# Gated MLP in three parts: the second product's accumulation gets a priority, and the third part rotates six tiles of stored weight combinations in place of four

## The chip, the cores and the metric

The kernel runs on one core of one Trainium2 chip. The metric is the device time of one execution in microseconds (us); the time before is the median of three runs.

## The reference, cut to what matters

The layer mixes 2064 rows (16 meta tokens and 2048 inputs) with RWKV-7 heads and attention heads, adds the result to the stream, and applies a gated MLP with a causal convolution of width three. The change touches the MLP alone:

```
def conv_ffn(u, w_up, conv_w, conv_b, w_down):
    hid = u @ w_up                                   # (rows, 1024) @ (1024, 5632)
    hid = (hid * conv_w[0] + shift_right(hid, 1) * conv_w[1]
           + shift_right(hid, 2) * conv_w[2] + conv_b)
    gate, val = jnp.split(hid, 2, axis=-1)           # 2816 each
    return (jax.nn.silu(gate) * val) @ w_down        # (rows, 2816) @ (2816, 1024)

h = h + conv_ffn(rms_norm(h, norm2_w[layer]), w_up[layer], ...)
return h[:, N_META:]
```

## The kernel before

Phase one (mixers and output projection) fills about half of the time and is not touched. Phase two, the MLP, works through the 2048 rows in three **parts** (`PARTS = [384, 384, 256]`); a part is two halves of that many rows, so the third part has 512 rows. All products are in float32 split into a high and a low tile, so that one product is three matmuls per 128 of its inner dimension (`mm3`).

Within a part, a loop runs over 22 column tiles **f** of the hidden layer, gate and value together. For each f the first product (`up_products`) is computed as seven products of half size, on combinations of the four quarters of the weights and of the input (Strassen's scheme in Winograd's form). The program calls them 0 to 6 by operand; on TensorE they stand in the order 0, 1, 4, 3, 5, 6, 2 and are written P0, P1, P4, P3, P5, P6, P2 here. One product is 12 matmuls into one PSUM bank (tag `up`, 4 banks). Its weights lie in a tile `o` of 128 x 1024 float32 (high and low half, 512 KB), and all `o` tiles share a rotation of `OPB` = 4 buffers:

- P0, P1 and P6 use quarters of the raw weights: `wraw` is loaded (512 KB for the first tile, 256 KB for the second, lines 1048 and 1050), ScalarE rounds it to the high half (line 1068) and GpSimd subtracts to get the low half (line 1069).
- P4, P3, P5 and P2 use combinations. The first part computes them and stores the finished `o` tiles in DRAM (`kept`); the second and third part only load them (line 1066).

VectorE and ScalarE combine the seven results, apply the convolution and the gate, and write `gh` and `gl`. The weights of the second product come as `wraw` too (line 152), and ScalarE and GpSimd split them into `dh` and `dl` (lines 155, 156), one buffer for each of two tags' halves.

The second product (`down`) takes two f at a time: after the up products of f = 2, 4, 6 and so on, TensorE runs the 48 matmuls `dn` of the two f before, six for each bank of 128 x 512, and VectorE adds each bank to the running sum `acc` (line 1031).

Operand tiles of the inputs (`ah`, `al`, seven each, `PARTS[i] + 2` columns wide) sit in a pool of their own that is closed and opened again when the part's size changes, so that in the third part they take 57,792 bytes of a partition where they took 86,464 before. Between the parts (here called the **transition**) the last `down` of a part is computed beside the loading, transposing and combining of the next part's input; its sums go out (line 1033) and the next part's `acc` tiles come in (line 983).

All DMAs are issued by SyncE (SP) in one order. The order of every engine is set by a scheduler that builds a timeline ahead of the run and takes, among what is ready, the instruction of the lowest priority number; matmuls of the products are pinned to the order in which they are written. A rotation of n buffers means that an `o` tile's load, or its rounding on ScalarE, waits until TensorE has finished the product that stands n places before it.

Of the kernel before, what the change touches and what calls it, by code (L numbers as in the profile page):

```python
# [9 lines left out]
F32R = mybir.dt.float32r  # L10
I32 = mybir.dt.int32
AF = mybir.ActivationFunctionType
ALU = mybir.AluOpType
# [23 lines left out]
PARTS = [384, 384, 256]  # L37
HMAX = max(PARTS)

UB, TWB, RAWB, OPB, GHB, TB, CB, DB = 2, 5, 3, 4, 3, 2, 1, 2  # L40
WBUF, QKB = 5, 2
GN = 256


# [47 lines left out]
class K:  # L92
# [222 lines left out]
    def begin(self, g):  # L315
# [3 lines left out]

        xh = sp.tile([128, 8, GN], F32R, tag="xh", name="xh")  # L320
        xl = sp.tile([128, 8, GN], F32R, tag="xl", name="xl")
        if n < GN:
            nc.gpsimd.memset(xh[:, :, n:].bitcast(F32), 0.0)
# [12 lines left out]
    def outputs(self, tag, bufs):  # L336

        return [self.sp.tile([128, 4, GN], F32R, tag=tag + p, name=tag + p, bufs=bufs) for p in "hl"]

# [45 lines left out]
    def duo(self, d):  # L385

        sp, nch = self.sp, self.nch
        return dict(
            gt=sp.tile([128, 2, GN], F32, tag=f"gt{d}", name="gt"),
            gb=sp.tile([128, 2, GN], F32, tag=f"gb{d}", name="gb"),  # L390
            wc=sp.tile([128, 2, 4], F32, tag=f"wc{d}", name="wc"),
# [550 lines left out]
    def phase2(self):  # L942


        tc, nc, a = self.tc, self.nc, self.a
        V, A, P = nc.vector, nc.scalar, nc.gpsimd
        cols = self.cols
        self.qa, self.qf = Queue(tc), Queue(tc)
        with ExitStack() as es:
            pool = lambda name, bufs=1, **kw: es.enter_context(tc.tile_pool(name=name, bufs=bufs, reuse_waits="tile", **kw))  # L950
            up = pool("u2")
            self.psum = Pools(pool("dn2", 4, space=PSUM), up=(pool("up2", 4, space=PSUM), "up"))
            nw = up.tile([128, D], F32, name="nw")
            nc.sync.dma_start(nw, a["n2"].unsqueeze(0).to_broadcast([128, D]))

            self.halo = up.tile([128, 2, 2, 4, 2], F32, name="halo")

            self.tail = up.tile([128, NFT, 2, 2], F32, name="tail")

            self.kp, self.kept = es.enter_context(tc.tile_pool(name="kp2", bufs=1, space=DRAM)), {}  # L960
            wp, sp = pool("w2"), pool("s2")
            lp, ac = pool("l2", side="right"), pool("a2", side="right")
            oes = es.enter_context(ExitStack())

            def operands(i):

                if i and PARTS[i] == PARTS[i - 1]:
                    return ops
                oes.close()
                op = oes.enter_context(tc.tile_pool(name="o2", bufs=1, reuse_waits="tile"))  # L970
                return [[op.tile([128, 4, PARTS[i] + 2], F32R, name=f"a{p}{o}") for p in "hl"] for o in range(7)]

            ops = operands(0)
            dpool = Pools(lp, up=(wp, "wraw"))
            r0 = 0
            self.begin2(0, 0, up, nw, ops)
            for i, half in enumerate(PARTS):
                N = half if i else half + 2
                nb = half // 64
                acc = []  # L980
                for b in range(nb):
                    acc.append(ac.tile([128, D], F32, tag=f"acc{b}", name=f"acc{b}"))
                    nc.sync.dma_start(acc[b], self.h2[r0 + 2 + b * 128:r0 + 130 + b * 128])
                grp = []
                for f in range(NFT):
                    gh = lp.tile([128, 2 * HMAX], F32R, tag="gh", name="gh", bufs=GHB)
                    gl = lp.tile([128, 2 * HMAX], F32R, tag="gl", name="gl", bufs=GHB)
                    cs = self.up_products(f, N, up, wp, sp, ops)
                    for t in range(2):
                        ts = []  # L990
                        for z in range(2):
                            c = cs[2 * t + z]
                            o = sp.tile([128, HMAX], F32, tag=f"t{z}", name=f"t{z}", bufs=TB)[:, 0:half]
                            j = 2 * f + z
                            A.activation(o, c[:, 2:half + 2], AF.Identity, bias=cols[:, C_CB + j:C_CB + j + 1],  # L995
                                         scale=cols[:, C_CW0 + j:C_CW0 + j + 1])
                            V.scalar_tensor_tensor(o, c[:, 1:half + 1], cols[:, C_CW1 + j:C_CW1 + j + 1], o,  # L997
                                                   op0=ALU.mult, op1=ALU.add)
                            V.scalar_tensor_tensor(o, c[:, 0:half], cols[:, C_CW2 + j:C_CW2 + j + 1], o,  # L999
                                                   op0=ALU.mult, op1=ALU.add)  # L1000
                            ts.append(o)
                        A.activation(ts[0], ts[0], AF.Silu)
                        V.tensor_tensor(ts[0], ts[0], ts[1], op=ALU.mult)
                        hs = slice(t * half, t * half + half)
                        A.activation(gh[:, hs], ts[0], AF.Copy)  # L1005
                        P.tensor_tensor(gl[:, hs], ts[0], gh[:, hs].bitcast(F32), op=ALU.subtract)  # L1006
                    grp.append((gh, gl, self.wsplit(dpool, a["wdn"][f], [128, 1024], "d", RAWB, DB)))
                    if f == NFT - 1:
                        if i == len(PARTS) - 1:
                            self.down(grp[:-1], acc, r0, False)  # L1010
                            grp = grp[-1:]
                        if i < len(PARTS) - 1:
                            ops = operands(i + 1)
                            self.begin2(i + 1, r0 + 2 * half, up, nw, ops)
                        self.down(grp, acc, r0, True)
                    elif len(grp) == 3:
                        self.down(grp[:2], acc, r0, False)
                        grp = grp[2:]
                r0 += 2 * half

    def down(self, grp, acc, r0, last):

        nc = self.nc
        for b, t in enumerate(acc):
            bs = slice(b * 128, b * 128 + 128)
            for h in range(2):
                hs = slice(h * 512, h * 512 + 512)
                ps = self.psum.tile([128, 512], F32, tag="dn", name="dn")
                for e, (gh, gl, (wh, wl)) in enumerate(grp):
                    self.mm3(ps, gh[:, bs], gl[:, bs], wh[:, hs], wl[:, hs], e == 0, e == len(grp) - 1)  # L1030
                nc.vector.tensor_tensor(t[:, hs], t[:, hs], ps, op=ALU.add)  # L1031
            if last:
                nc.sync.dma_start(self.out[r0 + b * 128:r0 + b * 128 + 128], t)

    def up_products(self, f, N, up, wp, sp, ops):


        nc = self.nc
# [21 lines left out]

        def product(o, w):

            t = wp.tile([128, 2, 4, 128], F32R, tag="o", name="o", bufs=OPB)
            hi, lo = t[:, 0], t[:, 1]
            if w is None:
                nc.sync.dma_start(t.bitcast(F32), self.kept[o, f])
            else:
                A.activation(hi, w, AF.Copy)  # L1068
                P.tensor_tensor(lo, w, hi.bitcast(F32), op=ALU.subtract)  # L1069
                if o in (2, 3, 4, 5):  # L1070
                    d = self.kept[o, f] = self.kp.tile([128, 2, 4, 128], F32, tag=f"k{o}_{f}", name="kept2")
                    nc.sync.dma_start(d, t.bitcast(F32))
            ps = self.psum.tile([128, 512], F32, tag="up", name="up")[:, 0:N]
            xh, xl = ops[o]
            for k in range(4):
                self.mm3(ps, hi[:, k, :], lo[:, k, :], xh[:, k, 0:N], xl[:, k, 0:N], k == 0, k == 3)
            return ps
# [13 lines left out]
        t1 = comb(b12, b11)  # L1091
        t2 = comb(b22, t1)
        p1 = product(0, b11)
        tu, u = tile_("cu")
        A.activation(u, p1, AF.Copy)
        p2 = product(1, b21)
        t11, c11 = tile_("c11")
        before(t11, tail[:, 0])
        tt(c11, p2, u, op=add)
        p6 = product(4, t2)  # L1100
        tt(u, p6, u, op=add)
        p5 = product(3, t1)
# [125 lines left out]
```

## Time and profile before

| | |
|---|---|
| median of 3 runs | 3096.91 us (3095.21 to 3106.47) |
| the profiled execution | 3101.82 us, span 3100.0 us |
| granted TensorE clock over the span | 0.953 of full speed |
| TensorE, VectorE, ScalarE, GpSimd busy | 91%, 68%, 38%, 36% |
| HBM traffic | 484 MB read, 99 MB written |

The span begins with the first instruction and ends with the last; times of rows count from its start. A busy share is a mean over stages that are limited by different things, so that the rows below are taken from the stretch that the change touches.

### The profile page before, as it was taken

The page shows a single profiled execution, that of the slowest core. Times are in us where ns is not written, and L with a number is a line of the kernel's source. Part 1 is how long each engine was busy: PE and PEld are TensorE (multiplying, and loading weights), DVE is VectorE, ACT ScalarE, POOL GpSimd, SP SyncE. Part 2 cuts the span into 40 slices and gives each one's busy share as a digit, 9 for nine tenths or more (in the row PEclk, how much of TensorE's full clock was granted, in tenths as well). Part 3 has the DMA queues.
Part 4 walks back from the last instruction along what each step waited for, and adds up shares of the span by engine and source line. Part 5 has one row for each costly group of instructions (what it writes and reads, how often), then busy time and mean ns, then how long its engine had stood idle before and what let it go on. Part 6 is the DMA issues. An engine that isn't in the chain of part 4 may idle for free.

```text
span 3100.0 us, 55199 instructions
## 1 busy us (share of the span) xinstructions
PE 2834.1 (91%) x19749; PEld 2396.3 (77%) x19749; DVE 2105.8 (68%) x6008; ACT 1188.0 (38%) x2758; POOL 1107.3 (36%) x1246
## 2 busy tenths in 40 slices
PE   6789898989999999999859999999899999989998
PEld 5567586777777776777548898888899999888887
DVE  5576766667666766666758878787655655766666
ACT  3344433334343433333234443434433333433343
POOL 3322311111111111111146665656444444554554
PEclk8799999989999999999969999999999999999999
DMA  6676677557676767776754343434644444565564
GB/s 216 211 213 187 208 233 233 179 166 231 183 242 183 242 186 226 194 228 192 246 209 156 146 153 133 156 129 162 232 149 139 155 156 140 189 215 177 201 212 159
DMA packets 302198, 586.43 MB, mean 189 GB/s; under 512 B 150570, under 2 KB 154266, under 8 KB 301924
## 3 DMA queue, kind: packets, MB, share of 16 engines
q1 hardware_dynamic: 301924, 582.90, 58.0%
q8 instruction: 157, 2.57, 0.3%
q14 instruction: 117, 0.96, 0.1%
HBM read 483.98 MB, written 98.79 MB: 188 GB/s over the span
## 4 chain that ended last, share of the span: by engine, by line
PE 61%; DVE 15%; DMA 13%; issue 3%; ACT 3%; SPq 3%; POOL 1%; DVEq 0%; ACTq 0%; POOLq 0%
PE up L86 17%; PE dn L86 13%; PE g L86 12%; PE o L86 5%; DMA o<-kept 4%; PE po L86 3%; SPq L587 2%; DMA wraw<-in_wup 2%; PE ma L86 2%; DVE t L997 2%; PE ps L86 2%; DVE tw L1058 2%; DMA w<-kept 2%; DVE t L999 1%; DMA nt<-nd 1%
## 5 line engine op out<-in xcount | busy, mean ns | idle before, releaser
L86 PE MATMUL up<-ah,o 128*128 128x386 f32 (+2 forms) x3696 | 882.7, 324 | 49.9 <-DMA o<-kept 29.0
L86 PEld LDWEIGHTS up<-ah,o 128*128 128x128 f32 x3696 | 652.4, 192 | 61.6 <-issue 11.6
L86 PE MATMUL up<-al,o 128*128 128x386 f32 (+2 forms) x1848 | 596.9, 323 | 6.9 <-DVE al L913 6.9
L86 PE MATMUL g<-xh,w 128*128 128x256 f32 x2016 | 425.8, 301 | 18.7 <-ACT w L170 7.3
L86 PEld LDWEIGHTS g<-xh,w 128*128 128x128 f32 x2016 | 334.7, 198 | 51.6 <-issue 19.8
L86 PEld LDWEIGHTS up<-al,o 128*128 128x128 f32 x1848 | 354.8, 192 | 8.8 <-DVE al L913 7.7
L1031 DVE TENSOR_TENSOR acc<-acc,dn 128x512 f32<-128x512 f32 x360 | 242.4, 684 | 114.9 <-PE dn L86 113.9
L86 PE MATMUL dn<-dh,gh 128*128 128x512 f32 x704 | 279.7, 397 | 29.0 <-DVE acc L1031 26.4
L1069 POOL TENSOR_TENSOR o<-wraw,o 128x512 fp32r<-128x512 f32 x198 | 269.5, 1361 | 99.0 <-ACT o L1068 72.2
L86 PE MATMUL g<-xl,w 128*128 128x256 f32 x1008 | 300.2, 298 | 3.1 <-DVE xl L145 3.1
L86 PE MATMUL dn<-dh,gl 128*128 128x512 f32 x704 | 276.6, 393 | 0.7 <-POOL gl L1006 0.7
L86 PE MATMUL dn<-dl,gh 128*128 128x512 f32 x704 | 276.3, 393 | 0.0
L156 POOL TENSOR_TENSOR dl<-wraw,dh 128x1024 fp32r<-128x1024 f32 x66 | 158.7, 2424 | 203.3 <-ACT dh L155 203.3
L997 DVE SCALAR_TENSOR_TENSOR t<-c,cols,t 128x384 f32<-128x384 f32 (+1 forms) x198 | 169.7, 858 | 79.5 <-ACT t L995 77.4
L86 PEld LDWEIGHTS g<-xl,w 128*128 128x128 f32 x1008 | 199.7, 198 | 14.6 <-issue 6.6
L1006 POOL TENSOR_TENSOR gl<-t,gh 128x384 fp32r<-128x384 f32 (+1 forms) x132 | 134.8, 1021 | 145.4 <-ACT gh L1005 145.4
L592 DVE TENSOR_TENSOR tm<-nt,tt 128x60 f32<-128x60 f32 (+36 forms) x558 | 128.9, 231 | 83.2 <-DMA w<-kept 28.3
L86 PEld LDWEIGHTS dn<-dh,gh 128*128 128x128 f32 x704 | 133.1, 189 | 65.4 <-DVE acc L1031 36.0
L676 POOL TENSOR_TENSOR sw<-S,wc 128x128 f32<-128x128 f32 x66 | 28.5, 432 | 421.1 <-DVE S L677 314.8
L1068 ACT ACTIVATE o<-wraw 128x512 fp32r<-128x512 f32 x198 | 121.8, 625 | 132.4 <-PE up L86 117.5
L995 ACT ACTIVATE t<-c,cols 128x384 f32<-128x384 f32 (+1 forms) x198 | 125.9, 667 | 106.9 <-DVE c L1112 102.1
L86 PE MATMUL g<-w,xh 128*128 128x256 f32 (+3 forms) x544 | 151.7, 362 | 13.9 <-ACT w L170 8.3
(283 smaller groups left out, 5672.3 us busy)
## 6 DMA issues: line engine op xcount, KB each, us to landing
w<-kept SPq DMA_DIRECT2D x448, 512.0 KB
o<-kept SPq DMA_DIRECT2D x176, 512.0 KB
wraw<-in_wup SPq DMA_DIRECT2D x88, 512.0 KB
kept<-o SPq DMA_DIRECT2D x88, 512.0 KB
wraw<-in_wdn SPq DMA_DIRECT2D x66, 512.0 KB
kept<-w SPq DMA_DIRECT2D x56, 512.0 KB
wraw<-in_wup SPq DMA_DIRECT2D x44, 256.0 KB
xt<-in_x SPq DMA_DIRECT2D x16, 512.0 KB
```

The costliest lines, as they stand in the source:

```text
L86: self._pin(self.nc.tensor.matmul(*args, **kw))
L156: nc.gpsimd.tensor_tensor(lo, raw, hi.bitcast(F32), op=ALU.subtract)
L587: nc.sync.dma_start(nt[p0:p0 + H], ndv[:, b * 32:b * 32 + 32, b * 32:b * 32 + 32])
L592: V.tensor_tensor(t, bc(nt[0:np_, s, s + 1:32], j, 1), tt[0:np_, 0:j, s:s + 1].to_broadcast([np_, j, m]), op=ALU.mult)
L995: A.activation(o, c[:, 2:half + 2], AF.Identity, bias=cols[:, C_CB + j:C_CB + j + 1], scale=cols[:, C_CW0 + j:C_CW0 + j + 1])
L997: V.scalar_tensor_tensor(o, c[:, 1:half + 1], cols[:, C_CW1 + j:C_CW1 + j + 1], o, op0=ALU.mult, op1=ALU.add)
L999: V.scalar_tensor_tensor(o, c[:, 0:half], cols[:, C_CW2 + j:C_CW2 + j + 1], o, op0=ALU.mult, op1=ALU.add)
L1006: P.tensor_tensor(gl[:, hs], ts[0], gh[:, hs].bitcast(F32), op=ALU.subtract)
L1031: nc.vector.tensor_tensor(t[:, hs], t[:, hs], ps, op=ALU.add)
L1058: V.tensor_tensor(t, x, y, op=ALU.subtract)
L1068: A.activation(hi, w, AF.Copy)
L1069: P.tensor_tensor(lo, w, hi.bitcast(F32), op=ALU.subtract)
```

## The change

Two edits. The VectorE add of a `down` bank into `acc` is issued under a priority raised by 400. And the tiles `o` of the third part, the only one that is smaller than `HMAX`, are taken from the pool of the operand tiles, in a rotation of six; the four buffers of the first two parts stay where they are and idle in the third.

```
+DOWN = 400
...
                 op = oes.enter_context(tc.tile_pool(name="o2", bufs=1, reuse_waits="tile"))
+
+                self.oplace = (op, OPB + 2) if PARTS[i] < HMAX else (wp, OPB)
                 return [[op.tile([128, 4, PARTS[i] + 2], F32R, name=f"a{p}{o}") for p in "hl"] for o in range(7)]
...
-                nc.vector.tensor_tensor(t[:, hs], t[:, hs], ps, op=ALU.add)
+                with self.tc.high_priority(DOWN):
+                    nc.vector.tensor_tensor(t[:, hs], t[:, hs], ps, op=ALU.add)
...
-            t = wp.tile([128, 2, 4, 128], F32R, tag="o", name="o", bufs=OPB)
+            pool, bufs = self.oplace
+            t = pool.tile([128, 2, 4, 128], F32R, tag="o", name="o", bufs=bufs)
```

What this does to the order of instructions: nothing moves on any engine before the transition from the second to the third part. There, VectorE's adds change places with neighbours by a few rows; in the rounds after it VectorE's order is the same as before but for a few rows of the first two f. TensorE's matmuls differ only in where 8 of the 32 transposes of the transition stand. The rest moves on ScalarE, GpSimd and SP in the third part. Line numbers of the changed kernel are one to five higher.

SP at the transition: `o_29835`, `o_29851`, `o_29869` and `o_29904` are the loads for P4, P3, P5 and P2 of the third part's first f, `wraw_29956` and `wraw_29958` the raw weights of its second f, `out` the sums that leave and `acc` those that come in. Before:

```order
L1066 DMA o_29835<-kept2_19919 128x1024
L1048 DMA wraw_29956<-in_wup 128x1024
L1066 DMA o_29851<-kept2_19938 128x1024
L891 DMA u_29632<-h2_60 128x1024
L891 DMA u_29645<-h2_60 128x1024
L1033 DMA out_0<-acc0_25013 128x1024
...
L1033 DMA out_0<-acc5_25023 128x1024
L1066 DMA o_29869<-kept2_19960 128x1024
L1050 DMA wraw_29958<-in_wup 128x512
L1066 DMA o_29904<-kept2_20000 128x1024
```

Now:

```order
L1071 DMA o_29835<-kept2_19919 128x1024
L1071 DMA o_29851<-kept2_19938 128x1024
L892 DMA u_29632<-h2_60 128x1024
L1071 DMA o_29869<-kept2_19960 128x1024
L892 DMA u_29645<-h2_60 128x1024
L1052 DMA wraw_29956<-in_wup 128x1024
L1054 DMA wraw_29958<-in_wup 128x512
L1037 DMA out_0<-acc0_25013 128x1024
...
L1037 DMA out_0<-acc5_25023 128x1024
L1071 DMA o_29904<-kept2_20000 128x1024
```

The load for P5 and the second half of the raw weights moved from behind the six outgoing sums to ahead of them.

GpSimd at the transition: `o_29798`, `o_29816` and `o_29887` are the low halves for P0, P1 and P6 of the third part's first f; `gl_29388` is one of the low halves that the last `down` of the second part needs. Before:

```order
L1069 TENSOR_TENSOR o_29798<-wraw_29794,o_29798 128x512
L1119 COPY tail_19620<-c22_29479 128x2
L1069 TENSOR_TENSOR o_29816<-wraw_29794,o_29816 128x512
L1085 COPY c22_29479<-c12_29461 128x2
L1118 COPY tail_19620<-cu_29409 128x2
L1085 COPY c12_29866<-tail_19620 128x2
L1006 TENSOR_TENSOR gl_29388<-t0_29519,gh_29387 128x384
```

Now:

```order
L1124 COPY tail_19620<-c22_29479 128x2
L1090 COPY c22_29479<-c12_29461 128x2
L1123 COPY tail_19620<-cu_29409 128x2
L1074 TENSOR_TENSOR o_29798<-wraw_29794,o_29798 128x512
L1074 TENSOR_TENSOR o_29816<-wraw_29794,o_29816 128x512
L1090 COPY c12_29866<-tail_19620 128x2
L1074 TENSOR_TENSOR o_29887<-wraw_29796,o_29887 128x512
L1009 TENSOR_TENSOR gl_29388<-t0_29519,gh_29387 128x384
```

Two conversions moved behind the copies, a third one came in, and all three now stand right ahead of `gl`.

GpSimd in a round of the third part, from the end of a `down` on: `o_30437` is for P6 of the f that now begins (A), `o_30510`, `o_30528` and `o_30599` are for P0, P1 and P6 of the next (B). Before:

```order
L156 TENSOR_TENSOR dl_30275<-wraw_30272,dh_30274 128x1024
L156 TENSOR_TENSOR dl_30501<-wraw_30498,dh_30500 128x1024
L1085 COPY cu_30364<-c11_30382 128x2
L1069 TENSOR_TENSOR o_30437<-wraw_30346,o_30437 128x512
L1085 COPY c11_30544<-tail_19620 128x2
L1069 TENSOR_TENSOR o_30510<-wraw_30506,o_30510 128x512
L1119 COPY tail_19620<-c22_30434 128x2
L1069 TENSOR_TENSOR o_30528<-wraw_30506,o_30528 128x512
```

Now:

```order
L157 TENSOR_TENSOR dl_30275<-wraw_30272,dh_30274 128x1024
L157 TENSOR_TENSOR dl_30501<-wraw_30498,dh_30500 128x1024
L1090 COPY cu_30364<-c11_30382 128x2
L1074 TENSOR_TENSOR o_30510<-wraw_30506,o_30510 128x512
L1074 TENSOR_TENSOR o_30528<-wraw_30506,o_30528 128x512
L1090 COPY c11_30544<-tail_19620 128x2
L1124 COPY tail_19620<-c22_30434 128x2
```

The conversion for A's P6 left this place (it is done before the `down` now), and those for B's P0 and P1 follow directly on the two `dl`.

## Rows read from the trace of the kernel before

**Rows 1.** The page's head and its busy times by engine.

```profile
span 3100.0 us, 55199 instructions
...
PE 2834.1 (91%) x19749; PEld 2396.3 (77%) x19749; DVE 2105.8 (68%) x6008; ACT 1188.0 (38%) x2758; POOL 1107.3 (36%) x1246
```

**Rows 2.** Chain that ended last, third part: start, length, what, how many.

```profile
2706.22 2.68 PE up L86 x23
2708.90 6.39 DMA o<-kept
2715.43 6.92 PE up L86 x36
...
2748.14 10.90 PE dn L86 x48
...
3023.96 4.53 PE up L86 x36
...
3062.42 10.93 PE dn L86 x48
3073.34 8.60 PE up L86 x72
```

**Rows 3.** Groups of instructions, 2740 to 3080 us: busy, mean; idle before, its releasers.

```profile
L86 PE MATMUL up<-ah,o 128*128 128x256 f32 x1079 | 205.9, 288 | 28.3 <-DMA o<-kept 24.2 <-DVE cu L1101 1.9 <-DVE t L1003 1.0
```

**Rows 4.** TensorE in order of time: start, length; in brackets idle before, releaser.

```profile
2688.32 0.51 PE L86 MATMUL dn<-dh,gl 128*128 128x512 f32 x1 [0.35 <-POOL gl L1006]
...
3004.90 0.28 PE L86 MATMUL up<-ah,o 128*128 128x256 f32 x1
...
3014.40 0.36 PE L86 MATMUL up<-ah,o 128*128 128x256 f32 x1 [0.75 <-DMA o<-kept]
...
3021.38 0.36 PE L86 MATMUL up<-ah,o 128*128 128x256 f32 x1 [1.03 <-DVE t L1003]
...
3023.96 0.36 PE L86 MATMUL up<-ah,o 128*128 128x256 f32 x1 [0.92 <-DMA o<-kept]
```

**Rows 5.** SP's DMA issues in one round, in order of time.

```profile
2994.19 12.65 SPq L1066 DMA_DIRECT2D o<-kept  x2
...
3009.41 0.32 SPq L1066 DMA_DIRECT2D o<-kept  x1
...
3013.67 2.75 SPq L1066 DMA_DIRECT2D o<-kept  x2
...
3017.52 3.18 SPq L1066 DMA_DIRECT2D o<-kept  x2
```

**Rows 6.** Stretches: busy PE, PEld, DVE, ACT, POOL; granted clock, DMA share, GB/s.

```profile
2683.00:2707.00 24.00, 22.20 (x115) 17.93 (x114) 23.63 (x37) 12.47 (x22) 14.58 (x13) 1.00 0.68 250
2706.22:2748.14 41.92, 34.88 (x253) 34.16 (x253) 23.77 (x45) 17.07 (x34) 22.90 (x32) 0.88 0.71 246
3006.00:3007.00 1.00, 1.00 (x11) 1.00 (x10) 0.00 (x0) 0.81 (x2) 1.00 (x1) 1.00 0.00 0
3007.00:3014.40 7.40, 6.65 (x57) 6.47 (x55) 4.96 (x8) 2.91 (x6) 6.25 (x6) 1.00 0.86 276
3007.00:3023.96 16.96, 14.26 (x116) 13.73 (x115) 11.21 (x20) 7.17 (x15) 11.91 (x16) 1.00 0.89 297
3008.00:3026.00 18.00, 15.30 (x125) 14.77 (x124) 12.94 (x23) 7.71 (x16) 12.02 (x15) 1.00 0.83 288
3026.00:3041.00 15.00, 15.00 (x84) 13.11 (x84) 9.75 (x20) 5.63 (x11) 5.33 (x9) 1.00 0.31 106
```

**Rows 7.** GpSimd in order of time, at the transition and in the round.

```profile
2685.26 0.42 POOL L1085 COPY c<-tail 128x2 f32<-128x2 f32 x1 [0.64 <-DVE t L999]
2687.26 1.00 POOL L1006 TENSOR_TENSOR gl<-t,gh 128x384 fp32r<-128x384 f32 x1 [1.59 <-ACT gh L1005]
...
3005.55 4.82 POOL L156 TENSOR_TENSOR dl<-wraw,dh 128x1024 fp32r<-128x1024 f32 x2 [4.96 <-ACT dh L155]
3010.31 0.38 POOL L1085 COPY cu<-c 128x2 f32<-128x2 f32 x1
3010.65 1.29 POOL L1069 TENSOR_TENSOR o<-wraw,o 128x512 fp32r<-128x512 f32 x1
```

## The prediction

> **What bounds the kernel now.** TensorE is busy for 91% of the span [rows 1], so time is to be had where it stands still. Nothing moves before the transition to the third part, so I read the chain that ended last from there on. It is a train of TensorE work with loads of stored combinations in it. The first up products of the third part start at 2706.22, its first `dn` block at 2748.14, its last but one at 3062.42 [rows 2]: between those two blocks lie nine rounds of two f each, (3062.42 - 2748.14) / 9 = 34.92 us a round.
>
> What would a round take if TensorE never waited? Six products in a row took 8.60 us (72 matmuls), or 1.433 us for one; a `dn` block takes 10.90 us [rows 2]. Fourteen products and a block make 20.07 + 10.90 = 30.97 us. So 3.95 us of each round are lost, 35.6 us in nine. The stretch ahead of them, 2706.22 to 2748.14, holds 21 products, 30.1 us; it took 41.92, so it lost 11.8 us. Together 47.4 us are the most that this change can give back, since the block at the end and all that follows 3073 does not hang on loads.
>
> The groups of instructions say who was waited for: 28.3 us of idle time stand ahead of the up matmuls from 2740 to 3080, 24.2 of them ended by a load of `o` [rows 3]. In the round from 3004.90 on there are three stops, before P2 of its first f (A), and before P3 and P5 of its second (B), at 3014.40, 3021.38 and 3023.96 [rows 4]. The middle one is put down to a VectorE multiply that no product waits for, so I count it to the load issued for P3. The rest of the 3.95 us is the start after each stop (36 matmuls in 4.53 us where three products in a row take 4.30 [rows 2]) and a few stretches at half clock.
>
> Why are the loads late? With four buffers, the load for a product is issued when the product four places ahead is done, so three products, 4.3 us, lie between its issue and its use. P2 of A was issued at 3009.41 and could start at 3014.40, P5 of B at 3017.52 and 3023.96 [rows 4, 5]: 5.0 and 6.4 us. The DMA engines are the reason: 0.83 busy at 288 GB/s from 3008 to 3026, then nearly idle, 106 GB/s from 3026 to 3041, while the `dn` block runs [rows 6].
>
> **The change part by part.** *The priority of the adds.* It moves no add in the rounds; VectorE's order there is the same. In the transition VectorE is busy 23.63 of 24 us whatever its order [rows 6], so trading neighbours gives or costs no more than one add or multiply, under 1 us. I take 0.
>
> *Six buffers in the rounds.* A load now follows the product six places ahead: five products, 7.17 us, lie between issue and use. Nothing is added: the same 13 transfers of 512 KB, 0.524 MB, pass per round (eight loads of `o`, three in all for the raw up weights, two for the second product). What moves is where they pass. Before, ten went from A's P0 to B's P5: A's P5 and P2 loads, B's raw weights (1.5), its second-product weights `wdn` (1), B's four loads and the next raw weights (1.5); 10 x 0.524 = 5.24 MB is what 18 us at 288 GB/s carry, 5.18 [rows 6]. Now A's P5 load and B's first raw weights go ahead of or beside the `dn` block, which has room. From `wdn` on, the queue holds in this order: `wdn`, P4 and P3 of B, the next raw weights, P5 of B, P2 of B.
>
> How long until the fifth of them is there? The rows give a rule of thumb. The DMA engines were idle until 3007, after the load issued at 2994.19 + 12.65 - 0.32 = 3006.52 [rows 5, 6]: I take 1.1 us from issue to first bytes. When A's P2 was released at 3014.40, 7.40 us x 276 = 2.04 MB had passed, though it stood third (1.57 MB); when B's P5 was released at 3023.96, 16.96 x 297 = 5.04 MB, though 8.5 transfers (4.46 MB) reach to its end [rows 4, 6]. So a load is usable once its own bytes, all ahead of it and some 0.53 MB more have passed. The Trainium skill, "DMA: Bandwidth & Descriptors", section "Queues, rings and completion order", says that on each DMA engine the descriptors of one ring are taken in order, though a later one may finish first; that alone would count no bytes from behind. The trace shows the 0.53 MB more, and I go by the trace; by the rule the sum is that of the first rival.
>
> In the worked round `wdn` can go when GpSimd has split the second `dl`, at 3005.55 + 4.82 = 3010.4 [rows 7], first bytes at 3011.5. B's P5 needs 5 x 0.524 + 0.53 = 3.15 MB, 10.9 us at 288 GB/s: 3022.4. TensorE wants it eleven products after 3004.90, at 3020.7. It is 1.7 us late, with one start of 0.2 us: 1.9 lost in place of 3.95. The others by the same rule: A's P2, issued at 3006.5, is there at 3011.3 and wanted at 3013.5; B's P4 at 3017.0, wanted 3017.8; B's P3 at 3018.8, wanted 3019.2. All in time, the last two narrowly. Gain 2.05 x 9 = **18.5 us**. Its ends: 3.95 x 9 = 35.6 if nothing is late, and 1.4 if the queue runs at the 246 GB/s of the stretch 2706 to 2748 [rows 6] (12.8 us, 3.6 late, 3.8 lost).
>
> *The transition.* P5's load of the first f was issued at 2708.90, behind the outgoing sums, and TensorE, whose first four products end at 2706.22 + 5.73 = 2711.95, stood until 2715.43 and then ran 36 matmuls in 6.92 us where 4.30 are normal [rows 2] (granted clock 0.88 over this stretch, a mean of its two levels, 2.4 GHz and 1.2 [rows 6]). Now the load goes ahead of the sums, with some 20 us to spare. Gain 3.5 + 2.6 = **6.1 us**. The other 5.7 us of this stretch I leave: three f without a block between them ask for 6.5 transfers in 10.0 us, 340 GB/s, more than any row shows over such a time. Bounds 0 (the stop goes to the next load) and 11.8.
>
> Against it stands GpSimd: three conversions of 1.29 us now go ahead of `gl`, where it had 0.64 and 1.59 us idle [rows 7], and the last `down` of part two waits for that `gl` at 2688.32 [rows 4]. So `gl` comes up to 3.87 - 2.23 = 1.6 us later; VectorE, full at 23.63 of 24 us, hides it in part if its adds come later anyway. Bounds 0 and 1.6; I take **0.8 us**, the middle. If VectorE's slack is gone it is all 1.6.
>
> Sum: 18.5 + 6.1 - 0.8 = 23.8 us off the profiled 3101.82, or 3078.0. That execution lies 4.9 us above the median of the runs, so the forecast for the median is 3096.9 - 23.8 = **3073 us**, 0.8% faster.
>
> **The rivals.** *Nothing is late any more.* If bytes from behind don't hold a load back, B's P5 needs 2.62 MB, 9.1 us: 3020.6, just in time, and the half-clock stretches go too. 47.4 - 0.8 off: about 3050. For it: all margins are short of zero by under 2 us. Against: 0.47 and 0.58 MB extra in both loads that I could count.
>
> *The loads stay the limit.* The two products' lead brings more transfers into flight at once, and what is won at the issue is lost in the queue. For it: the engines are 0.83 to 0.89 busy in these 18 us already [rows 6]. At 246 GB/s the rounds give 1.4 us, and with 6.1 - 1.6 from the transition that makes 3091; with a gain up to 15.5 us I count it here.
>
> *Slower.* SP issues in order. The next raw weights now stand ahead of B's P5 load and wait for GpSimd's conversion for B's P1. By the rows this is done at 3010.65 + 2 x 1.29 = 3013.2 [rows 7], just before A's P6 ends at 3004.90 + 6 x 1.433 = 3013.5 and frees the buffer. Each microsecond that GpSimd is later there delays B's P5 load by one. From 2.7 us a round on (23.8 / 9) all gain is gone; at 4.4 us it costs 0.5%, 3112. GpSimd has no more work than before, so this would take slower instructions on it.
>
> *Half of the change does nothing:* the priority. That is in the forecast already.
>
> **How the numbers follow.** Chances: the forecast (15.5 to 33 us gained) 0.53, nothing late 0.13, loads stay the limit 0.27, slower or no gain by the queue's order 0.07, of which 0.05 beyond 0.5%. A measurement of this kernel can tell about 0.5%, 15.5 us, from no change; so faster 0.66, same 0.29, slower 0.05. The range reaches into both neighbours, 3052 to 3092, and leaves out the slower cases and the tails of the two others.
>
> **What would show it.** Right: rounds of 32.9 us; idle time ahead of the up matmuls half of 28.3; A's P2 without a stop, B's P5 with one of some 1.5 us; the first f of the third part without its stop of 3.5 us; the DMA engines busier in the `dn` blocks than 106 GB/s; VectorE's adds where they were. Wrong: three stops a round as before with longer times from issue to use; or a wait for VectorE or GpSimd where the load's wait was; or `gl` holding the last `down` of part two for more than 2 us.

## The result, and the profile after

| | before | after |
|---|---|---|
| median | 3096.91 us | 3074.27 us (3061.59 to 3080.77) |
| the profiled execution | 3101.82 us, span 3100.0 | 3080.77 us, span 3079.0 |

The ratio is 0.9906, 95% interval 0.988 to 0.9931: some 29 us faster (21 to 37); the two medians differ by 22.6 us. The forecast was 3073 us, 23.8 us off the profiled execution.

The page of after, head and busy times by engine [rows 1]: TensorE's work is the same, VectorE is busy 30 us longer with the same 6008 instructions.

```profile
span 3079.0 us, 55147 instructions
...
PE 2837.5 (92%) x19749; PEld 2400.5 (78%) x19749; DVE 2135.8 (69%) x6008; ACT 1187.5 (39%) x2758; POOL 1106.5 (36%) x1246
```

The chain that ended last, third part (start, length, what, how many) [rows 2]:

```profile
2721.63 2.61 PE up L87 x22
2724.24 8.21 DMA o<-kept
2732.59 1.70 PE up L87 x12
...
2757.84 10.90 PE dn L87 x48
2768.74 20.06 PE up L87 x168
2788.80 10.91 PE dn L87 x48
2799.71 20.06 PE up L87 x168
2819.77 10.90 PE dn L87 x48
...
2851.43 10.91 PE dn L87 x48
...
3041.41 10.90 PE dn L87 x48
```

The nine rounds took (3041.41 - 2757.84) / 9 = 31.51 us each, where they took 34.92. The first two are TensorE's work alone: 168 up matmuls in 20.06 us and a block of 10.90. Later ones are 31.66 us, and the chain shows why: no load stands in them any more. The groups of instructions for 2740 to 3080 [rows 3], and TensorE in order of time (idle before and its releaser in brackets) [rows 4], say what stands there:

```profile
L87 PE MATMUL up<-ah,o 128*128 128x256 f32 x1144 | 209.7, 284 | 5.3 <-ACT cu L1100 5.3
```

```profile
2699.38 0.50 PE L87 MATMUL dn<-dh,gh 128*128 128x512 f32 x1 [2.90 <-ACT gh L1008]
2701.45 0.80 PE L87 MATMUL dn<-dh,gl 128*128 128x512 f32 x1 [1.33 <-POOL gl L1009]
...
2732.59 0.36 PE L87 MATMUL up<-ah,o 128*128 128x256 f32 x1 [2.37 <-DMA o<-kept]
2743.21 0.39 PE L87 MATMUL up<-ah,o 128*128 128x256 f32 x1 [3.23 <-ACT cu L1100]
...
3005.00 0.39 PE L87 MATMUL up<-ah,o 128*128 128x256 f32 x1 [0.27 <-ACT cu L1100]
```

Idle time ahead of the up matmuls fell from 28.3 to 5.3 us, and none of the 5.3 is put down to a load. Of it, 3.2 us are the stop at 2743.21, ahead of the first `dn` block; the other 2.1 lie in seven of the nine rounds. What is left in a round is one stop, ahead of B's P5, for `cu`: ScalarE's eviction of B's P0, whose PSUM bank P5 takes over (four banks, four products). The two first stops lie in the transition and are longer than before (2.90 us for `gh` after 1.3, 1.33 for `gl` after 0.35).

**Where the time went, stretch by stretch.** From the last block of up products of part two to the first up product of part three it is 2679.28 to 2721.63, 42.35 us; before it was 2668.70 to 2706.22, 37.52. So the transition lost 4.8 us. From there to the first `dn` block it is 36.21 us after 41.92: 5.7 won. The rounds won 9 x 3.41 = 30.7. That makes 31.6 us between these two executions; e1 below shows how far the parts move by chance. The spans differ by only 21.0, because the execution of after already came 10.6 us later to the start of this stretch, with the same instructions behind it; the runs below show that this is chance. I therefore compare stretches of traces below, from the start of that last block of up products (84 matmuls in the chain) to the tenth `dn` block of 48, and call it the **changed stretch**: 393.7 us before (2668.70 to 3062.42), 362.1 after (2679.28 to 3041.41).

The stretches of after (busy PE, PEld, DVE, ACT, POOL; granted clock, DMA share, GB/s) [rows 6]:

```profile
2721.63:2757.84 36.21, 30.60 (x253) 30.22 (x253) 25.17 (x43) 15.23 (x32) 22.54 (x30) 1.00 0.81 291
2995.42:3004.00 8.58, 8.58 (x74) 8.58 (x74) 7.60 (x13) 3.13 (x7) 4.56 (x9) 1.00 0.98 371
3010.00:3021.00 11.00, 11.00 (x52) 9.15 (x52) 9.10 (x17) 4.39 (x9) 4.21 (x6) 1.00 0.40 144
```

And SP's issues in one round, from `wdn` on [rows 5]: P4 and P3 of B in the second row, the next raw weights in the third, P5 and P2 of B in the fourth:

```profile
2994.32 0.33 SPq L153 DMA_DIRECT2D wraw<-in_wdn  x1
2994.76 1.73 SPq L1071 DMA_DIRECT2D o<-kept  x2
2997.18 0.33 SPq L1052 DMA_DIRECT2D wraw<-in_wup  x1
2997.61 3.19 SPq L1071 DMA_DIRECT2D o<-kept  x2
```

The order in the queue is the one forecast. The rate is not: with the queue full for 8.6 us, 371 GB/s passed at a DMA share of 0.98.

### The profile page after: what moved, and what is told of

It reads as the page before. It is cut to its first block, busy times and chain, and to the rows that moved or that the text cites. A ratio compares the mean times of both kernels' runs of the same rounds, so it can differ in the third digit from the quotient of the medians.

```text
span 3079.0 us, 55147 instructions
## 1 busy us (share of the span) xinstructions
PE 2837.5 (92%) x19749; PEld 2400.5 (78%) x19749; DVE 2135.8 (69%) x6008; ACT 1187.5 (39%) x2758; POOL 1106.5 (36%) x1246
## 4 chain that ended last, share of the span: by engine, by line
PE 62%; DVE 16%; DMA 10%; issue 4%; ACT 3%; SPq 2%; POOL 1%; DVEq 0%; ACTq 0%; POOLq 0%
PE up L87 16%; PE g L87 14%; PE dn L87 13%; PE o L87 5%; PE po L87 3%; DVE t L1000 3%; DMA wraw<-in_wup 2%; PE ma L87 2%; DMA w<-kept 2%; PE ps L87 2%; DVE t L1002 2%; DVE tw L1062 2%; SPq L588 2%; PE sc L87 1%; DMA nt<-nd 1%
## 5 line engine op out<-in xcount | busy, mean ns | idle before, releaser
L87 PE MATMUL up<-ah,o 128*128 128x386 f32 (+2 forms) x3696 | 871.5, 322 | 26.2 <-ACT cu L1100 13.0
L87 PEld LDWEIGHTS up<-ah,o 128*128 128x128 f32 x3696 | 645.1, 190 | 34.6 <-ACT cu L1100 17.8
L1000 DVE SCALAR_TENSOR_TENSOR t<-c,cols,t 128x384 f32<-128x384 f32 (+1 forms) x198 | 162.2, 821 | 71.3 <-ACT t L998 69.8
L1002 DVE SCALAR_TENSOR_TENSOR t<-c,cols,t 128x384 f32<-128x384 f32 (+1 forms) x198 | 180.6, 934 | 1.1
```

What stands on the lines that cost most here:

```text
L87: self._pin(self.nc.tensor.matmul(*args, **kw))
```

## The experiments

Each was timed against the kernel before on the same chip. Ratios are to that kernel, the other columns from the profiled execution: the first from the start of the last block of up products of part two to the first `dn` block of 48 matmuls, then the mean of the nine rounds, then both together, the changed stretch.

| kernel | ratio, 95% interval | to first block | round | changed stretch |
|---|---|---|---|---|
| before | | 79.4 | 34.92 | 393.7 |
| after | 0.9906 (0.988 to 0.9931) | 78.6 | 31.51 | 362.1 |
| e1 priority alone | 0.9992 (0.9971 to 1.0012) | 75.7 | 34.53 | 386.5 |
| e3 five buffers | 0.9898 (0.9867 to 0.9929) | 72.8 | 31.95 | 360.3 |
| e4 a load twice | 0.9908 (0.988 to 0.9937) | 78.6 | 31.93 | 366.0 |
| e5 `gl` ahead | 0.9875 (0.985 to 0.9901) | 71.3 | 31.44 | 354.2 |
| e6 `cu` first | 0.9885 (0.9856 to 0.9913) | 78.1 | 31.21 | 359.0 |
| e7 low halves on VectorE | 0.9892 (0.9862 to 0.9922) | 76.9 | 31.19 | 357.6 |
| e8 = e5 + e6 | 0.985 (0.9824 to 0.9876) | 70.8 | 31.44 | 353.8 |
| e9 = e5 + e6 + e7 | 0.987 (0.9838 to 0.9901) | 69.0 | 31.23 | 350.1 |
| e10 = e9, seven buffers | 0.9875 (0.9843 to 0.9908) | 68.6 | 31.15 | 349.0 |

**e1: the priority alone, four buffers.** On every engine the order of instructions is that of the kernel before; and with six buffers and no priority it is that of after. So nothing of the change is the priority's.

```
-                self.oplace = (op, OPB + 2) if PARTS[i] < HMAX else (wp, OPB)
+                self.oplace = (wp, OPB)
```

> Four buffers as before, and the raised priority of the adds kept. Theory: the priority gives nothing, since the order of instructions on all engines is that of the kernel before; rounds of 34.9 us, ratio 0.997 to 1.003. Rival: the adds come earlier after all and a part of the gain is theirs; then rounds under 34 us and a ratio under 0.997. Beside it: in the two profiled executions the last block of up products of part two started at 2668.70 us before and at 2679.28 after, with the same instructions ahead of it. If that is chance, it starts here anywhere between 2660 and 2685; if the change made it, at 2669.

Measured: ratio 0.9992, rounds of 34.53 us. The rival is out. The run also tells what chance does to one program: its changed stretch is 7.2 us shorter than that of before, 3.7 of them ahead of the first `dn` block. From the first up product to that block (columns as in [rows 6]):

```profile
2715.38:2753.61 38.23, 30.75 (x254) 30.20 (x253) 23.60 (x45) 17.22 (x34) 22.67 (x31) 1.00 0.77 268
```

Before took 41.92 us there at a granted clock of 0.88. e1 has the same stop for the load of P5 (3.29 us), but its clock stays at 1.00. Against e1, after's changed stretch is 24.4 us shorter, not 31.6: 27.2 won in the rounds, 2.0 in the stretch ahead of them, 4.8 lost in the transition, which is 37.51 us in e1. And e1's last block of up products began at 2677.87, where before had 2668.70 and after 2679.28. Over all eleven profiled executions this start lies between 2663.64 (e6) and 2679.72 us (e5), with the same order of instructions on TensorE ahead of it. So the 10.6 us are chance, and single executions of the whole kernel tell a few us of difference badly.

**e3: five buffers.**

```
-                self.oplace = (op, OPB + 2) if PARTS[i] < HMAX else (wp, OPB)
+                self.oplace = (op, OPB + 1) if PARTS[i] < HMAX else (wp, OPB)
```

> Five buffers in the third part in place of six. Theory: what counts is the time between a load's issue and its use, four products or 5.73 us here; before, P2 of the first f took 5.0 us and P5 of the second 6.4 us, so that the first is in time and the second late by at most 0.7 us: rounds of 31.3 to 32.4 us, ratio 0.990 to 0.993. Rival: the loads are limited by the mean rate of the queue (288 GB/s), and each buffer gives its share: rounds of 33.3 us, halfway between four and six, ratio 0.995.

Measured: rounds of (3038.60 - 2751.09) / 9 = 31.95 us, ratio 0.9898. The view of waits of TensorE, 2751 to 3050 (in all, times, longest):

```profile
PE up L87 <- DMA o<-kept: 1.7, 3, 1.1
PE up L87 <- POOL o L1074: 1.4, 2, 0.9
PE up L87 <- ACT cu L1100: 1.2, 5, 0.3
```

Loads stop TensorE three times in nine rounds, once for 1.1 us where 0.7 at most were expected. One buffer more, which lengthens the lead from three products to four, is nearly the whole gain. The time from issue to use decides, as the theory had it, and not each buffer with a share of its own: halfway between four and six would have been 33.2.

**e4: how much slack six buffers leave, and the queue's rate.**

```
-        nc.sync.dma_start(raw, src)
+        first = nc.sync.dma_start(raw, src)
+        if tag == "d" and self.third:
+            again = self.third.tile(shape, F32, tag="again", name="again", bufs=1)
+            second = nc.sync.dma_start(again, src)
...
```

(`self.third` is the pool of the operand tiles in the third part; the second load is tied behind the first in SP's order. In the round from 2992 on, P4's load stands between the two, which leaves the bytes ahead of P5 the same.)

> Six buffers as after, but in the third part each second-product weight block is loaded a second time, into a tile that nobody reads, right behind the first: 0.524 MB more ahead of the second f's P3 and P5 loads. From the first bytes of the first of the two loads to the last needed for P5, 3.15 MB become 3.67 MB. Theory (the queue, once it is full, passes 367 GB/s, and 0.53 MB from behind hold a load back): 10.0 us, where TensorE leaves 9.3 to 9.6: late by 0.4 to 0.7 us, rounds of 32.0 to 32.5 us. Rival 1 (288 GB/s, as forecast): 12.7 us, 3.1 us late, rounds of 34.5 us. Rival 2 (367 GB/s and no bytes from behind): 8.6 us, in time, rounds as after, 31.7 us.

Measured: rounds of (3039.39 - 2752.01) / 9 = 31.93 us. The waits of TensorE, 2752 to 3050, and four of the stops in order of time:

```profile
PE up L87 <- DMA o<-kept: 5.3, 8, 1.0
```

```profile
2808.67 0.36 PE L87 MATMUL up<-ah,o 128*128 128x256 f32 x1 [0.36 <-DMA o<-kept]
2811.24 0.36 PE L87 MATMUL up<-ah,o 128*128 128x256 f32 x1 [0.93 <-DMA o<-kept]
...
2936.93 0.36 PE L87 MATMUL up<-ah,o 128*128 128x256 f32 x1 [0.86 <-DMA o<-kept]
...
3003.45 0.36 PE L87 MATMUL up<-ah,o 128*128 128x256 f32 x1 [0.47 <-DMA o<-kept]
```

Stops for loads are back, eight in nine rounds, 0.2 to 1.0 us each: the size that 367 GB/s with bytes from behind gives, not the 3.1 us that 288 GB/s would, and not none. They do not come in every round, so that the mean is a little under the band. A ninth stop, of 0.89 us, is put down to ScalarE's `gh`, which no up product reads; P5's load reported its landing 0.13 us before it ended. After's loads were therefore in time by less than the 1.4 us that 0.524 MB take at 367 GB/s.

In the round of the last row above, from the first bytes of `wdn` at some 2994 to the release of P5 (columns as above):

```profile
2994.00:3003.45 9.45, 8.98 (x76) 8.80 (x75) 8.19 (x15) 3.87 (x9) 4.90 (x9) 1.00 0.99 395
```

That is 3.73 MB where 3.15 reach to P5's end, 0.58 more, beside 0.47 and 0.58 in the two loads of the kernel before. The packed trace, from which the views are made, hints at what these bytes are. Each load reports its landing by 16 marks. Those of P5's load lie here between 3002.15 and 3003.31, 1.2 us in which 0.46 MB pass at 395 GB/s; those of a load with an empty queue ahead of it (before, issued at 3006.52) lie within 0.3 us. So the load seems to wait for the last of its 16 parts while others already carry what stands behind; no run tells this from a fixed time of some 1.4 us.

In after, the last mark of P5's load comes 0.4 to 0.9 us before TensorE is there in eight of nine rounds. In the ninth (2941.70) it comes 0.3 us too late, beside the end of `cu` (2941.76), to which that stop of 0.42 us is put down. Six buffers leave little slack.

**e5: the transition.** GpSimd's conversions for the third part's first f are tied behind the last `gl` of part two.

```
-                        P.tensor_tensor(gl[:, hs], ts[0], gh[:, hs].bitcast(F32), op=ALU.subtract)
+                        self.lastgl = P.tensor_tensor(gl[:, hs], ts[0], gh[:, hs].bitcast(F32), op=ALU.subtract)
...
-                P.tensor_tensor(lo, w, hi.bitcast(F32), op=ALU.subtract)
+                ins = P.tensor_tensor(lo, w, hi.bitcast(F32), op=ALU.subtract)
+                if f == 0 and pool is not wp:
+                    self.tc.add_manual_dep(ins.ins, self.lastgl.ins.name, ...)
```

> As after, but GpSimd's conversions for the third part's first f are held behind the last gl of part two. Theory: in the transition these conversions delayed gl and stretched VectorE's multiply-adds beside them, and TensorE stood 2.90 us for gh and 1.33 us for gl; without them both stops fall to under 1 us together, and the time from the last block of up products of part two to the first product of part three falls from 42.35 us to about 38 (37.52 before). Rival: that time is set by the combining of the new input on VectorE and ScalarE, and stays at 41 to 43 us; or the first product then waits for the held conversions, with a new stop of 1 to 3 us ahead of P0 or P1.

Measured: from 2679.72 to the first up product at 2716.36, 36.64 us (42.35 after, 37.52 before); e4 and e6, which leave the conversions where after has them, took 42 and 41 us, and e8 to e10, which share this edit, 36 to 37. The stops are 0.81 us for `gh` and 0.36 for `gl`. The theory holds, and no new stop came. GpSimd and then VectorE of after, at this place, in order of time [rows 7]:

```profile
2695.16 3.20 POOL L1074 TENSOR_TENSOR o<-wraw,o 128x512 fp32r<-128x512 f32 x2
2698.31 0.51 POOL L1090 COPY c<-tail 128x2 f32<-128x2 f32 x1
2698.78 1.66 POOL L1074 TENSOR_TENSOR o<-wraw,o 128x512 fp32r<-128x512 f32 x1
2700.41 0.99 POOL L1009 TENSOR_TENSOR gl<-t,gh 128x384 fp32r<-128x384 f32 x1
```

```profile
2695.07 2.16 DVE L1002 SCALAR_TENSOR_TENSOR t<-c,cols,t 128x384 f32<-128x384 f32 x2
2697.16 1.62 DVE L1006 TENSOR_TENSOR t<-t,t 128x384 f32<-128x384 f32 x1
2698.70 0.61 DVE L1000 SCALAR_TENSOR_TENSOR t<-cu,cols,t 128x384 f32<-128x384 f32 x1
2699.23 0.68 DVE L918 TENSOR_TENSOR tw<-tp,tw 128x512 f32<-128x512 f32 x1
```

And VectorE of e5:

```profile
2695.51 1.14 DVE L1002 SCALAR_TENSOR_TENSOR t<-c,cols,t 128x384 f32<-128x384 f32 x2
2696.57 0.55 DVE L1006 TENSOR_TENSOR t<-t,t 128x384 f32<-128x384 f32 x1
```

Beside the conversions the two multiply-adds took 2.16 us in place of 1.14, the product (line 1006) 1.62 in place of 0.55, and its end sets `gh`: 2.1 us, which is the difference of the `gh` stops, 2.90 - 0.81. The third conversion, 1.66 us, stood ahead of `gl`: 1.33 - 0.36 = 1.0. Line 918, which reads one of its inputs from PSUM, ran beside that conversion in its usual 0.68 us. The Trainium skill, "SBUF — State Buffer", section "Who interferes with whom", says that a VectorE instruction with two inputs in SBUF contends with a GpSimd instruction that reads SBUF, and that one with at most one such input, outside the two-port modes, does not. The trace agrees: 1.62 us against 0.55 for the one, no change for the other.

**e6: the new stop in the rounds.** ScalarE in order of time, in a round of after:

```profile
3003.43 0.42 ACT L1008 ACTIVATE gh<-t 128x256 fp32r<-128x256 f32 x1 [2.29 <-DVE t L1006]
3003.75 0.62 ACT L1073 ACTIVATE o<-wraw 128x512 fp32r<-128x512 f32 x1
3004.28 0.40 ACT L1005 ACTIVATE t<-t 128x256 f32<-128x256 f32 x1
3004.58 0.36 ACT L1100 ACTIVATE cu<-up 128x256 f32<-128x256 f32 x1
```

The eviction has nothing to wait for (B's P0 ended some 4 us before); it stands behind `gh`, which waited 2.29 us for VectorE. The edit raises its priority, which here does change the order:

```
-        A.activation(u, p1, AF.Copy)
+        with ExitStack() as es:
+            if self.oplace[0] is not wp:
+                es.enter_context(self.tc.high_priority(DOWN))
+            A.activation(u, p1, AF.Copy)
```

> As after, but in the third part ScalarE's eviction of P0 (cu) is issued under the raised priority, which puts it ahead of the Silu that stood in front of it. Theory: the stop of 0.27 to 0.42 us ahead of the second f's P5 that is left in the rounds comes from this eviction standing in ScalarE's order behind work that waits for VectorE; the Silu takes 0.3 us, so that the stop goes or falls under 0.1 us, and the rounds fall from 31.51 us to 31.0 to 31.2. Rival: the eviction still stands behind gh, which waits for VectorE, and nothing changes: rounds of 31.4 to 31.7 us.

Measured: rounds of 31.21 us, just above the theory's band. The eviction now stands ahead of the Silu (line 1005). TensorE's waits from 2660 on show one stop for `cu`, of 1.5 us and ahead of the first `dn` block, where after had eight (5.3 us in all). A round is still 0.24 us above 30.97. ScalarE and TensorE of e6 in one round, at the border from P3 to P5 of B:

```profile
2986.44 0.37 ACT L1103 ACTIVATE cu<-up 128x256 f32<-128x256 f32 x1
```

```profile
2986.62 0.63 PE L87 MATMUL up<-ah,o 128*128 128x256 f32 x2
```

TensorE is through with P3 at 2986.76 (eleven products after 2971.00), the eviction ends at 2986.81, and the two matmuls across the border take 0.63 us in place of 0.40. So a rest of the wait for `cu`, some 0.2 us and too short for a row of its own in the waits, seems to be left; four of nine rounds have it. In two others TensorE stood at this place for P5's load, by its last mark, the longer time for 0.7 us.

**e7: GpSimd's conversions moved to VectorE, in the third part.**

```
-                P.tensor_tensor(lo, w, hi.bitcast(F32), op=ALU.subtract)
+                (P if pool is wp else V).tensor_tensor(lo, w, hi.bitcast(F32), op=ALU.subtract)
```

> As after, but in the third part the low halves of the raw up weights (66 subtractions of 128x512) are made on VectorE, not on GpSimd. Theory: VectorE's multiply-adds are stretched by GpSimd's work beside them (line 1002: mean 1.13 us after, 0.62 before; 0.48 alone), so without these conversions their mean falls to 0.7 us or less, VectorE's 224 us of the nine rounds stay at 210 to 235 though it does 54 more subtractions, and rounds fall to 31.0 to 31.3 us; the transition falls below 40 us, since no conversion holds VectorE or stands ahead of gl. Rival: the subtractions just add 0.7 to 1.05 us each to VectorE, 38 to 57 us in nine rounds, and the waits for VectorE and ScalarE grow: rounds above 31.8 us.

Measured: rounds of 31.19 us, with no stop for `cu` in them and two for loads (0.47 and 0.69 us), the transition 39.50 (2675.82 to 2715.32). The groups of instructions of 2757 to 3041 in after, and of 2757 to 3035 here:

```profile
L1002 DVE SCALAR_TENSOR_TENSOR t<-c,cols,t 128x256 f32<-128x256 f32 x54 | 59.3, 1126 | 0.3
```

```profile
L1074 DVE TENSOR_TENSOR o<-wraw,o 128x512 fp32r<-128x512 f32 x54 | 51.5, 954 | 2.7 <-ACT o L1073 1.8
...
L1002 DVE SCALAR_TENSOR_TENSOR t<-c,cols,t 128x256 f32<-128x256 f32 x53 | 25.2, 475 | 0.0
```

The nine rounds as one stretch, of after and here (VectorE is the third busy time):

```profile
2757.84:3041.41 283.57, 281.54 (x1945) 262.52 (x1945) 224.38 (x378) 122.78 (x234) 170.34 (x215) 1.00 0.62 218
```

```profile
2752.69:3033.37 280.68, 279.39 (x1945) 261.84 (x1945) 218.54 (x433) 122.86 (x235) 112.64 (x162) 1.00 0.63 220
```

The multiply-add fell from 1126 to 475 ns, and VectorE was busy for 218.5 us in place of 224.4, with 55 instructions more. The rival is out: what GpSimd took from VectorE cost more than its work does there.

**e8 to e10: what they make together.** e8 is e5's and e6's edit, e9 adds e7's from the second f on, e10 is e9 with `OPB + 3`.

> The conversions of the third part's first f held behind the last gl of part two, and the eviction cu ahead of the Silu, together, on top of after. Theory: both gains add, since they lie in different stretches: transition 36.6 us as with the first alone, rounds 31.0 to 31.2 us; 3 to 5 us less than with the first alone, ratio 0.985 to 0.990. Rival: the eviction's place gives nothing, and it is the first alone again: rounds 31.44 us.

> All three on top of after: the first f's conversions behind the last gl, the eviction cu ahead of the Silu, and the low halves of the third part's raw up weights on VectorE from the second f on. Theory: the transition stays at 36.7 us as with the first two, since its conversions remain on GpSimd behind gl, and the rounds fall to 31.0 to 31.2 us, so that some 2 to 4 us less are used than with two, ratio 0.982 to 0.987. Rival: VectorE's subtractions in the first stretch, 36 us long, delay the combinations there, and what the rounds gain is lost: first stretch above 36 us.

> The same with seven buffers, which is all that the room freed in the third part holds. Theory: in the rounds no load is late with six, so the rounds stay at 31.0 to 31.2 us; in the first stretch, where loads still stopped TensorE by 1 to 3 us, up to 2 us may go; all in all within 3 us of the same with six. Rival: earlier loads fill the queue ahead of others that are wanted sooner, and the first stretch or the rounds get longer by 2 us or more.

Measured: e8 has the transition of e5 (36.66 us) and the best ratio of all, the only one whose interval lies below that of after. Its rounds are mostly 31.2 us, but two stops ahead of P5, of 1.2 and 0.7 us and both for its load by the last mark, bring the mean to 31.44. That is a miss: it is the rival's figure, and the changed stretch is only 0.4 us shorter than e5's where 3 to 5 were expected. In e9 six of nine rounds take 30.97 us, TensorE's work alone; two stops for loads, 0.74 and 1.11 us, are in the others, and from the last block of up products to the first `dn` block it is 69.0 us, so that VectorE's subtractions cost nothing there. e10 has one stop for a load in its rounds, and its changed stretch, 349.0 us, is the shortest. The ratios of the three overlap, so their order in whole time is open. By the changed stretch all three beat after, by 8 to 13 us, where before and e1 lie 7.2 us apart by chance; e9 keeps 12.0 of the 15.5 us that its three edits gave singly.

## Why the prediction was right, and where its sizes were off

**The priority of the adds, 0:** right. The order of instructions does not know it, and e1 has 0.9992.

**The rounds, 18.5 us:** right in mechanism (loads issued two products earlier, the same order in the queue, no stop for A's P2), but mis-sized: 30.7 us between these two executions, 27.2 if e1's rounds of 34.53 stand for four buffers. The step that failed is B's P5, forecast 1.7 us late. It was in time in eight rounds of nine, because the rate was mis-sized: 288 GB/s was the mean of 18 us in which the queue stood partly empty (0.83 busy [rows 6]), waiting for SP's issues and not passing bytes. That the bytes asked for (5.24 MB) and those passed (5.18) agree tells the demand of those 18 us, not what could pass. A queue that is kept full, which is what six buffers make, passed 371 GB/s; my 3.15 MB then take 8.5 us and not 10.9. From the first bytes at some 2995.4 that is 3003.9, 0.8 us before TensorE came to P5 (3005.00 less its stop of 0.27); the last mark of this load is at 3003.87. Emptiness is not all of it. In the stretch for which I needed the rate, the kernel before shows this (columns as above):

```profile
3011.50:3022.40 10.90, 9.12 (x75) 8.77 (x74) 8.07 (x16) 5.10 (x11) 6.93 (x12) 1.00 0.94 322
```

That is 322 GB/s at a share of 0.94, 343 for a full one, where after has 379 by the same division; why after's transfers also ran a tenth faster while they ran stays open. Taken from this row the sum would have been 9.8 us, and P5 0.6 us late.

The 0.53 MB beyond a load's own end, the other half of the rule, stand as a size: e4's stops of 0.2 to 1.0 us need them. So the first rival's round nearly came about (one load in nine late), but for another reason than that rival gave. By the order of a ring alone, which I took from the Trainium skill, "DMA: Bandwidth & Descriptors", section "Queues, rings and completion order", e4 would have had no stops; its trace has eight. The Trainium skill states that order for each DMA engine by itself, so that e4 does not contradict it; the step from it to no bytes from behind was mine.

**What is left of the rounds** was not forecast: 0.5 us of each, a wait for `cu`, since VectorE, held up by GpSimd, now comes behind a TensorE that no longer waits for loads (e6, e7). In the nine rounds of before the same multiply-adds (line 999 there, 1002 in after) took 32.0 us where after needs 59.3, 27 of the 30 us by which VectorE is busier:

```profile
L999 DVE SCALAR_TENSOR_TENSOR t<-c,cols,t 128x256 f32<-128x256 f32 x54 | 32.0, 620 | 0.3
```

I had named a wait for VectorE or GpSimd in the place of the load's wait as a sign of being wrong; in this small form it came.

**The first stretch, 6.1 us:** 5.7 measured against before, 2.0 against e1. P5's load ahead of the outgoing sums took its stop away, as forecast. The 2.6 us for the clock were mis-sized: after has a granted clock of 1.00 where before had 0.88, but so has e1 with P5's stop still in it: of two executions with the same order of instructions one has this loss and one has not. And part of what P5's stop gave went to the next ones: 2.37 us for P2's load, which still goes behind the outgoing sums, and 3.23 for `cu`. I had left 5.7 us alone because no row showed 340 GB/s; the 371 GB/s of after take that reason away.

**The transition, a cost of 0.8 us:** the sign is right, the size is off: 4.8 us, beyond the bound of 1.6 and beyond what I named as wrong (`gl` above 2 us; it was 1.33, but `gh` 2.90). I had counted only the place of `gl` in GpSimd's order. The conversions also slowed VectorE beside them, which made `gh` late; e5 shows it by taking both away. The profile of before had the hint: its two multiply-adds had means of 0.64 and 0.84 us from 2740 to 3080, for work that takes 0.48 alone.

The sum, 23.8 us, against 31.6 in the traces (24.4 against e1), 29 by the ratio and 22.6 by the medians. That the median came within 1.3 us of the forecast is partly luck: the rounds gave 9 to 12 us more than I said, the transition took 4 more, and the first stretch gave up to 4 less. The rival of a limit at the loads has fallen (no stop in after's rounds is put down to one), and so has the slower case, though it was not far: GpSimd's conversions for B's P0 and P1 ended at 2994.61 + 2.54 = 2997.15, the raw weights went at 2997.18, and B's P5 load behind them at 2997.61, when its buffer came free. GpSimd, in order of time in that round of after, had 0.4 us to spare:

```profile
2994.61 2.54 POOL L1074 TENSOR_TENSOR o<-wraw,o 128x512 fp32r<-128x512 f32 x2
```

## What to carry to other kernels

A mean rate over a stretch in which the queue ran empty is no ceiling for the queue: take the rate from the microseconds in which its share is near 1. The lead of a load, in work between issue and use, is to be set against its time from issue to use; here one buffer more was nearly enough, and the second left 0.4 to 0.9 us of slack in most rounds. An instruction that moves ahead on GpSimd costs not only those behind it there but also VectorE's instructions beside it that read SBUF twice.

## What the runs showed of the hardware that I had not expected

VectorE's multiply-add of 128 x 256 took 475 ns on the mean where GpSimd made no low halves of up weights, and 1126 ns where it did (e7, after). And the start of the last block of up products of part two, behind the same instructions, moved by 16 us from one execution to the next (2663.64 to 2679.72), half of what the whole change is worth.
